# The AV products of two attentions as one group of matmuls, issued where the scores of a later one stand

## The chip, the cores and the metric

The kernel runs on one core of one Trainium2 chip. The metric is the device time of one execution in microseconds, lower is better. Engines are called as in the profile: PE is TensorE (PEld its weight loads), DVE VectorE, ACT ScalarE, POOL GpSimd, SP the queue of SyncE that issues most DMAs. PE multiplies a stationary operand of 128 rows and up to 128 columns, which a weight load puts in place, with a moving operand, and writes to PSUM: eight banks per partition, each of 2 x 256 float32.

## The reference, cut to what matters

A trunk of two layers over 256 positions of width 2048. In each layer one projection feeds a convolution group and an attention group, whose results are gated, concatenated, projected back and added; then an embedding of the layer, gated by the residual, is added. The change lies in the attention group: 16 query heads of width 64 on 4 key/value heads, a window of 128 positions, a bias by relative position, a sink logit per head.

```python
def reference(x, p, norm_g, w_in, ...):
    ...
        u = hn @ w_in[i]
        a_val, a_glu, a_z, q, k, v, b_z = jnp.split(u, offs, axis=-1)
        ...
        yb = _window_attention(q, k, v, bias_band, sink[i]) * jax.nn.silu(b_z)
        h = h + jnp.concatenate([ya, yb], axis=-1) @ w_out[i]
```

Within `_window_attention`:

```python
        s = jnp.einsum('bqkgd,bskd->bkgqs', qb, kb, ...) * scale + bias_band
        m = jnp.maximum(jnp.max(s, axis=-1), sink_f)
        e = jnp.exp(s - m[..., None])
        denom = jnp.sum(e, axis=-1) + jnp.exp(sink_f - m)
        pr = (e / denom[..., None]).astype(vb.dtype)
        return jnp.einsum('bkgqs,bskd->bqkgd', pr, vb)
```

The last line is the AV product, probabilities times values, and the product with `silu(b_z)` follows it.

## The kernel before

Activations lie with channels on the partitions and the 256 positions along the free axis. A projection works through blocks of 128 output columns. Weights come from memory as float32 and are split into two parts, high and low (`split`, L168 on ACT, L171 on DVE); activations are split likewise, and each product of a weight block and an activation block is three matmuls (`mm3`, L401 to L403) of 128x128 by 128x256. The unit of the schedule is a **half**: eight blocks of the contraction, 24 matmuls, one split weight buffer. Two output blocks share one PSUM bank, so a `pair` is four halves.

After each half `pump()` is called. It lets the convolution on DVE go on by some taps, and advances every generator in the list `side` by one `yield`, in the order in which they were put there. The engines PE, DVE and ACT run their instructions in the order in which the program issues them; what a generator issues at a pump therefore stands between two halves of the projection on PE.

Each layer has eight attentions (i = 0 to 7), each for two query heads, hh = 0 and 1. A loop over i in steps of two does a pair of projections for the gate `zb` (its silu is L678), a pair for the queries (`qq`, L685 and L686), and then puts attentions i and i + 1 into `side`, the second to begin four halves after the first. So an attention begins every four halves, and several are under way at a time. After the loop come four pairs of projections `za`, beside which the last attentions run. In halves counted from its beginning, an attention issues:

- 0: the load of its bias (L339, a DMA of POOL)
- 1: scores, eight matmuls into two banks `sc` (L633)
- 2: DVE adds the bias and finds the maxima (L639), ACT follows at 3 with the exponentials (L646), DVE at 4 with the reciprocals (L651), ACT at 5 with the scaling of the probabilities in `s` (L654, four instructions)
- 6: eight transposes of the probabilities into two banks `pt`, one for each hh (L660)
- 7: ACT copies the two banks into two tiles `ptt` (L664)
- 10 (8 for the last one, i = 7): AV, four matmuls in float32 into a bank `av`, of which it uses one half (L670). The values are the stationary operand, 128 rows by 64 columns; the output of hh = 0 goes to partitions 0 to 63 and that of hh = 1 to 64 to 127, so a matmul uses one half of the array's columns. The trace shows each float32 matmul as two instructions: eight per attention
- one half later: DVE multiplies the result into `zb[:, i, :]` (L673)

Step 10 of an attention is step 6 of the next one and step 2 of the one after. On PE the AV of one attention is followed at once by the transposes of the next.

Behind the `za` projections stand `finish` (which pumps until no attention is left), the sums for the normalisation of the convolution (`mean`, L710; `rv0c`, `rv1c`, small matmuls at L354), and the output projections (`o`) and gates (`g`).

Tiles come from pools; a tag with `bufs=n` rotates over n buffers, and a tile waits until the one that had its buffer is read out. The tag `ptt` has two buffers, the tag `u` three: the latter is used at a layer's beginning (`hn`) and in its gates (`hs`). All PSUM banks are one tag of eight buffers.

Of the kernel before, what the change touches and what calls it, by code (L numbers as in the profile page):

```python
# [10 lines left out]
F32 = mybir.dt.float32  # L11
# [6 lines left out]
P = 128  # L18
D = 2048
S = 256  # L20
# [4 lines left out]
HD = 64  # L25
# [44 lines left out]
def backwards(a):  # L70

    (ps, pn), (st, n) = a.ap
    return bass.AP(a.tensor, a.offset + st * (n - 1), [[ps, pn], [-st, n]])
# [56 lines left out]
def trunk_kernel(ctx: ExitStack, tc: tile.TileContext, xT, pT, wst, par, gain, relb, sinkp, onehot, out):  # L130
    nc = tc.nc
# [7 lines left out]
    wk = ctx.enter_context(tc.tile_pool(name="wk", bufs=2))  # L139
# [7 lines left out]
    def halves(t):  # L147
        return [t[:, 0], t[:, 1]]

    def bank(name):  # L150
        return ps.tile([P, 2, S], F32, tag="ps", name=name)
# [85 lines left out]
    def wait(n):  # L237
        for _ in range(n):
            yield
# [94 lines left out]
    def load_bias(i):  # L334

        t = wk.tile([P, 2, 3 * P], F32, name=f"bias{i}", tag="bias", bufs=2)
        base = fscr[2 * i:2 * i + 2, :]
        src = bass.AP(base.tensor, base.offset, [[1, P], [512, 2], [1, 3 * P]])
        nc.gpsimd.dma_start(t, src)  # L339
        return t  # L340
# [98 lines left out]
    for l in range(DEPTH):  # L439
# [32 lines left out]
        for q in range(4):  # L472
# [6 lines left out]
            for jj in range(0, 4, 2):  # L479
                j = 4 * q + jj  # L480
                b = bank("e")
                for x in range(2):
                    for k in range(2):
                        if l:
                            mm3(b[:, x, :], w[:, :, jj + x, k, :], pp[:, :, k, :], x == 0 and k == 0, k == 1)
                        else:
                            nc.tensor.matmul(b[:, x, :], raw[:, jj + x, k, :], pf[:, k, :], start=x == 0 and k == 0,
                                             stop=k == 1, skip_group_check=True)
# [62 lines left out]
        a, zb = halves(az)  # L551
# [62 lines left out]
        v = wk.tile([P, 2, W_KV], F32, name=f"v{l}", tag="v", bufs=1)  # L614
        for b in range(2):
            nc.scalar.copy(v[:, b, :], vb[b][:, 0, :])

        def attention(i, qq, after, l=l, v=v, zb=zb):
            t = i // 4
            yield from wait(after)  # L620
            bias = load_bias(i)
            yield
            nm = wk.tile([P, 2, 2], F32, name="nm", tag="nm")
            den = wk.tile([P, 2, 2], F32, name="den", tag="den")
            es = wk.tile([P, 2, 2], F32, name="es", tag="es")
            sk = sinkt[:, l * NQ + 2 * i:l * NQ + 2 * i + 2].unsqueeze(1).broadcast_to([P, 2, 2])
            each = [(b, hh) for b in range(2) for hh in range(2)]
            o = []
            for b in range(2):
                o.append(bank("sc"))  # L630
                for hh in range(2):
                    for x in range(2):
                        nc.tensor.matmul(o[b][:, hh, :], qq[:, hh, b * P:(b + 1) * P], keys[t][x][:, hh, :],  # L633
                                         start=hh == 0 and x == 0, stop=x == 1, skip_group_check=True)
            yield from wait(1 + AW[0])
            s = [wk.tile([P, 2, S], F32, name="s", tag="s", bufs=4) for b in range(2)]
            for b, hh in each:
                c = l * NQ + 2 * i + hh
                nc.vector.tensor_tensor_reduce(  # L639
                    out=s[b][:, hh, :], in0=o[b][:, hh, :], in1=backwards(bias[:, hh, b * P:b * P + S]),  # L640
                    scale=1.0, scalar=nsink[:, c:c + 1], op0=ALU.add, op1=ALU.min,
                    accum_out=nm[:, b, hh:hh + 1])
            nc.vector.tensor_add(es, nm, sk)
            yield
            for b, hh in each:
                nc.scalar.activation(s[b][:, hh, :], s[b][:, hh, :], AF.Exp, bias=nm[:, b, hh:hh + 1],  # L646
                                     scale=-1.0, accum_out=den[:, b, hh:hh + 1])
            nc.scalar.activation(es, es, AF.Exp)
            yield from wait(1 + AW[1])
            nc.vector.tensor_add(den, den, es)  # L650
            nc.vector.reciprocal(den, den)  # L651
            yield from wait(1 + AW[2])
            for b, hh in each:
                nc.scalar.activation(s[b][:, hh, :], s[b][:, hh, :], AF.Copy, scale=den[:, b, hh:hh + 1])  # L654
            yield from wait(1 + AW[3])
            o = [bank("pt") for hh in range(2)]
            for hh in range(2):
                for b in range(2):
                    for kt in range(2):
                        nc.tensor.transpose(o[hh][:, kt, b * P:(b + 1) * P], s[b][:, hh, kt * P:(kt + 1) * P], ident)  # L660
            yield
            pt = [wk.tile([P, 2, S], F32, name="ptt", tag="ptt") for hh in range(2)]
            for hh in range(2):
                nc.scalar.copy(pt[hh], o[hh])  # L664
            yield from wait(1 if i == 7 else 3)
            o = bank("av")
            for kt in range(2):
                for hh in range(2):
                    g = 2 * t + hh
                    nc.tensor.matmul(o[hh * HD:(hh + 1) * HD, 0, :], v[:, kt, g * HD:(g + 1) * HD], pt[hh][:, kt, :],  # L670
                                     start=(kt == 0), stop=(kt == 1))
            yield
            nc.vector.tensor_mul(zb[:, i, :], o[:, 0, :], zb[:, i, :])  # L673

        for i in range(0, 8, 2):

            b = pair(hg, f"zb{l}_{i}")
            nc.scalar.activation(zb[:, i:i + 2, :], b, AF.Silu)  # L678
            b = pair(hg, f"q{l}_{i}")

            qq = wk.tile([P, 4 * S + 32], F32R, name="qq", tag="qq")
            qq = qq[:, 0:4 * S].rearrange("p (x h s) -> p x h s", x=2, h=2)
            for hh in range(2):
                r, o = rows_of[hh], rows_of[1 - hh]
                nc.scalar.mul(qq[r, :, hh, :], b[r], -(HD ** -0.5))  # L685
                nc.vector.scalar_tensor_tensor(qq[o, :, hh, :], b[r], -(HD ** -0.5), qq[r, :, hh, :].bitcast(F32),  # L686
                                               ALU.mult, ALU.subtract)
            for x in range(2):
                side.append(attention(i + x, qq[:, x], 4 * x))
# [240 lines left out]
```

## Time and profile before

| | us |
|---|---|
| median of 3 runs | 942.69 |
| lowest, highest | 941.69, 943.29 |
| the profiled execution | 943.05 |
| its span, first to last instruction | 941.3 |
| mean granted TensorE clock | 0.996 |

The page of the profile gives busy time by engine, the chain of work that ended last, and groups of instructions by line, with the operand tiles named as out<-in. Other views of the same trace are used below: waits (who waited for whom: total, times, longest), the timeline (start, duration, engine, line, operation, count; neighbours of one group merged), the chain in order of time, and windows (busy time and count of instructions within stretches, with the granted clock, the DMA share and GB/s). Matmuls overlap each other, so their durations add up to more than the time that passes: the spacing of their starts tells what a stream costs.

### The profile page before, as it was taken

To read this page: it belongs to the slowest core of one execution; us is meant where nothing else is said; L and a number is where in the kernel's file an instruction comes from. 1 tells how busy PE (TensorE), PEld (TensorE's weight loads), DVE (VectorE), ACT (ScalarE), POOL (GpSimd) and SP (SyncE) were. 2 spreads that over 40 slices of the span, in tenths; PEclk is the share of its full clock that TensorE was granted. 3 is DMA by queue.
4 is the path that set the end of the run, shared out by engine and by line. 5 is a ranking of instruction groups with operands and counts; after the bars stand their busy time and mean duration, and the time that the engine had idled before them with its cause. 6 is when DMAs were issued, how large, how long until landed. Compare 5 with 4: busy or idle time off the path is not lost.

```text
span 941.3 us, 19132 instructions
## 1 busy us (share of the span) xinstructions
PE 928.9 (99%) x7968; PEld 912.3 (97%) x7968; DVE 767.9 (82%) x1290; ACT 550.3 (58%) x830; POOL 83.0 (9%) x79
## 2 busy tenths in 40 slices
PE   8999999999999999999999999999999999999995
PEld 7999999999999999999999999999999999999995
DVE  3999999998787786786679999999887877777663
ACT  4655455787874555554467445568778546445551
POOL 0023001010000000011102100000100000000111
PEclk9999999999999999999999999999999999999999
DMA  8674556555546456556545556566455554655532
GB/s 296 230 253 162 197 180 237 191 202 186 171 158 249 156 213 211 189 180 232 212 183 205 183 198 222 179 213 201 170 169 180 176 206 146 257 179 180 198 117 90
DMA packets 29011, 182.55 MB, mean 194 GB/s; under 512 B 3595, under 2 KB 4156, under 8 KB 9084
## 3 DMA queue, kind: packets, MB, share of 16 engines
q1 hardware_dynamic: 24284, 165.70, 49.7%
q0 software_dynamic: 3344, 12.88, 4.2%
q10 hardware_dynamic: 1296, 2.75, 0.8%
q8 instruction: 62, 1.02, 0.4%
q14 instruction: 25, 0.20, 0.1%
HBM read 177.09 MB, written 4.23 MB: 193 GB/s over the span
## 4 chain that ended last, share of the span: by engine, by line
PE 95%; DVE 2%; DMA 1%; ACT 1%; issue 0%; ACTq 0%; DVEq 0%
PE o L401 6%; PE o L402 6%; PE o L403 6%; PE ag L401 6%; PE g L403 6%; PE ag L403 6%; PE ag L402 6%; PE g L402 6%; PE g L401 6%; PE za L401 3%; PE za L403 3%; PE za L402 3%; PE zb L401 3%; PE zb L403 3%; PE zb L402 3%; PE q L401 3%
## 5 line engine op out<-in xcount | busy, mean ns | idle before, releaser
L171 DVE TENSOR_TENSOR w<-raw,w 128x1024 fp32r<-128x1024 f32 x306 | 374.4, 1232 | 101.4 <-ACT w L168 100.4
L168 ACT CAST w<-raw 128x1024 fp32r<-128x1024 f32 x308 | 316.2, 1046 | 156.6 <-PE ag L403 44.0
L565 DVE SCALAR_TENSOR_TENSOR cz<-az,pars,cz 128x241 f32<-128x241 f32 (+11 forms) x480 | 216.2, 500 | 1.0
L401 PE MATMUL ag<-hg,w 128*128 128x256 f32 x512 | 141.9, 277 | 0.0
L403 PE MATMUL g<-h,w 128*128 128x256 f32 x512 | 141.5, 276 | 0.0
L402 PE MATMUL ag<-hg,w 128*128 128x256 f32 x512 | 141.5, 276 | 0.0
L403 PE MATMUL ag<-hg,w 128*128 128x256 f32 x512 | 141.5, 276 | 0.0
L401 PE MATMUL g<-h,w 128*128 128x256 f32 x512 | 141.4, 276 | 0.0
L402 PE MATMUL g<-h,w 128*128 128x256 f32 x512 | 141.4, 276 | 0.0
L401 PEld LDWEIGHTS ag<-hg,w 128*128 128x128 f32 x512 | 96.1, 188 | 0.9 <-ACT w L168 0.8
L402 PEld LDWEIGHTS ag<-hg,w 128*128 128x128 f32 x512 | 96.2, 188 | 0.0
L402 PEld LDWEIGHTS g<-h,w 128*128 128x128 f32 x512 | 96.1, 188 | 0.0
L403 PEld LDWEIGHTS ag<-hg,w 128*128 128x128 f32 x512 | 96.1, 188 | 0.0
L401 PEld LDWEIGHTS g<-h,w 128*128 128x128 f32 x512 | 96.1, 188 | 0.0
L403 PEld LDWEIGHTS g<-h,w 128*128 128x128 f32 x512 | 96.1, 188 | 0.0
L401 PE MATMUL za<-hg,w 128*128 128x256 f32 x256 | 71.9, 281 | 0.0
L401 PE MATMUL q<-hg,w 128*128 128x256 f32 x256 | 71.9, 281 | 0.0
L401 PE MATMUL o<-yb,w 128*128 128x256 f32 x256 | 71.9, 281 | 0.0
L401 PE MATMUL zb<-hg,w 128*128 128x256 f32 x256 | 71.5, 279 | 0.0
L402 PE MATMUL q<-hg,w 128*128 128x256 f32 x256 | 71.4, 279 | 0.0
L403 PE MATMUL q<-hg,w 128*128 128x256 f32 x256 | 71.4, 279 | 0.0
L402 PE MATMUL o<-yb,w 128*128 128x256 f32 x256 | 71.3, 278 | 0.0
(227 smaller groups left out, 2273.0 us busy)
## 6 DMA issues: line engine op xcount, KB each, us to landing
raw<-in_wst SPq DMA_DIRECT2D x153, 1024.0 KB, 4.9
bias<-fscr POOLq DMA_DIRECT2D x16, 384.0 KB, 3.9
raw<-in_wst SPq DMA_DIRECT2D x4, 512.0 KB, 7.9
az<-in_xT POOLq DMA_DIRECT2D x4, 512.0 KB, 5.6
hscr<-e POOLq DMA_DIRECT2D x2, 1024.0 KB, 5.6
az<-hscr POOLq DMA_DIRECT2D x4, 512.0 KB, 5.4
x<-in_xT SPq DMA_DIRECT2D x3, 512.0 KB, 8.2
out_t<-og ACTq DMA_DIRECT2D x4, 256.0 KB, 3.0
```

Source lines behind the costliest of these rows:

```text
L168: nc.scalar.copy(hi, raw)
L171: nc.vector.tensor_sub(lo, raw, hi.bitcast(F32))
L401: nc.tensor.matmul(o, w[:, 0], x[:, 0], start=start, stop=False, skip_group_check=True)
L402: nc.tensor.matmul(o, w[:, 0], x[:, 1], start=False, stop=False, skip_group_check=True)
L403: nc.tensor.matmul(o, w[:, 1], x[:, 0], start=False, stop=stop, skip_group_check=True)
L565: nc.vector.scalar_tensor_tensor(acc[:, t, lo_:hi_], a[:, t, lo_ + s:hi_ + s], w(k), acc[:, t, lo_:hi_], ALU.mult, ALU.add)
```

## The change

AV is done for two attentions at a time. The transposed probabilities are handed over in a list, `probs`, one list per layer. An attention with even i ends after the copies. One with odd i takes both pairs of tiles from the list and issues eight AV matmuls (sixteen instructions) into one bank, the even attention into its first half and the odd one into its second; one DVE product of 128x512 replaces two of 128x256. The matmul that starts accumulation is flagged so only for the first attention, since the flag acts on the whole bank. The odd attention does this at its half 9 (8 for i = 7, as before), which is half 1, the scores, of the attention two later. The tiles `ptt` of odd attentions take the tag `u`.

```diff
+        probs = []
+
-        def attention(i, qq, after, l=l, v=v, zb=zb):
+        def attention(i, qq, after, l=l, v=v, zb=zb, probs=probs):
...
-            pt = [wk.tile([P, 2, S], F32, name="ptt", tag="ptt") for hh in range(2)]
+            pt = [wk.tile([P, 2, S], F32, name="ptt", tag="u" if i % 2 else "ptt", bufs=3 if i % 2 else 2)
+                  for hh in range(2)]
             for hh in range(2):
                 nc.scalar.copy(pt[hh], o[hh])
-            yield from wait(1 if i == 7 else 3)
+            probs.append(pt)
+            if i % 2 == 0:
+                return
+            yield from wait(1 if i == 7 else 2)
             o = bank("av")
-            for kt in range(2):
-                for hh in range(2):
-                    g = 2 * t + hh
-                    nc.tensor.matmul(o[hh * HD:(hh + 1) * HD, 0, :], v[:, kt, g * HD:(g + 1) * HD], pt[hh][:, kt, :],
-                                     start=(kt == 0), stop=(kt == 1))
+            for x in range(2):
+                pt = probs.pop(0)
+                for kt in range(2):
+                    for hh in range(2):
+                        g = 2 * t + hh
+                        nc.tensor.matmul(o[hh * HD:(hh + 1) * HD, x, :], v[:, kt, g * HD:(g + 1) * HD],
+                                         pt[hh][:, kt, :], start=x == 0 and kt == 0, stop=kt == 1,
+                                         skip_group_check=True)
             yield
-            nc.vector.tensor_mul(zb[:, i, :], o[:, 0, :], zb[:, i, :])
+            nc.vector.tensor_mul(zb[:, i - 1:i + 1, :], o, zb[:, i - 1:i + 1, :])
```

## The prediction

> **What bounds the kernel now.** I read the page first: busy time, then the chain that ended last.
>
> ```profile
> span 941.3 us, 19132 instructions
> PE 928.9 (99%) x7968; PEld 912.3 (97%) x7968; DVE 767.9 (82%) x1290; ACT 550.3 (58%) x830; POOL 83.0 (9%) x79
> PE 95%; DVE 2%; DMA 1%; ACT 1%; issue 0%; ACTq 0%; DVEq 0%
> ```
>
> TensorE (PE) is the bound: 99% busy, 95% of the chain. The waits of PE, all of them in the span, come next; the second row is the only one in the attention stage.
>
> ```profile
> PE warm L261 <- DVE zeros L258: 1.2, 1, 1.2
> PE sc L633 <- DVE qq L686: 0.3, 1, 0.3
> ```
>
> So no engine is to be relieved here. What counts is how PE's stream is spaced, and a busy share can't show that, since matmuls overlap. I therefore read start times in the timeline of PE. This is the second attention's AV with the third's transposes; columns are start, duration, what.
>
> ```profile
> 206.61 0.28 PE L402 MATMUL q<-hg,w 128*128 128x256 f32 x1
> 206.73 0.28 PE L403 MATMUL q<-hg,w 128*128 128x256 f32 x1
> 206.94 1.08 PE L670 MATMUL av<-ptt,v 128*64 128x256 f32 x8
> 207.95 1.09 PE L660 MATMUL pt<-ident,s 128*128 128x128 f32 x8
> 209.00 0.28 PE L402 MATMUL q<-hg,w 128*128 128x256 f32 x1
> ```
>
> Projection matmuls start 0.12 apart. The first AV one starts 0.21 behind its predecessor, not 0.12: a price for entering 64-column tiles ("128*64"). From 206.73 to the second projection matmul behind the group (209.00) are 2.27 us; two steps (0.23) would have passed anyway, so AV with transposes costs **2.04**. The same stage has transposes alone (first attention) and AV alone (last one):
>
> ```profile
> 179.10 0.28 PE L403 MATMUL q<-hg,w 128*128 128x256 f32 x1
> 179.22 1.04 PE L660 MATMUL pt<-ident,s 128*128 128x128 f32 x8
> 180.22 0.28 PE L402 MATMUL q<-hg,w 128*128 128x256 f32 x1
> ...
> 283.80 0.28 PE L403 MATMUL za<-hg,w 128*128 128x256 f32 x1
> 284.01 1.08 PE L670 MATMUL av<-ptt,v 128*64 128x256 f32 x8
> 285.25 0.28 PE L402 MATMUL za<-hg,w 128*128 128x256 f32 x1
> ```
>
> Transposes alone: 1.12 - 0.23 = **0.89**. AV alone: 1.45 - 0.23 = **1.22**.
>
> One more thing must be seen: **the step of PE's stream has two lengths**. The windows view, PE alone, over stretches that hold projections only; the x is the count of matmuls.
>
> ```profile
> 593.00:621.00 28.00, 28.00 (x240) 1.00 0.69 240
> 843.00:871.00 28.00, 28.00 (x249) 1.00 0.51 180
> ```
>
> The granted clock is 1.00 in both. About two counted matmuls only reach into a window, so a step lasts 28.00/247 = 0.1134 in one and 28.00/238 = 0.1176 us in the other. I call them short and long step. A half (24 matmuls, the unit of the schedule) takes 24 x 0.0042 = 0.10 us more at long step. Equal windows of 5.2 us through the attention stage:
>
> ```profile
> 183.00:188.20 5.20, 5.20 (x48) 1.00 0.63 195
> 197.60:202.80 5.20, 5.20 (x46) 1.00 0.71 244
> 211.70:216.90 5.20, 5.20 (x48) 1.00 0.51 191
> 225.70:230.90 5.20, 5.20 (x46) 1.00 0.90 280
> ...
> 278.60:283.80 5.20, 5.20 (x46) 1.00 0.59 208
> 287.00:292.20 5.20, 5.20 (x49) 1.00 0.66 255
> 297.60:302.80 5.20, 5.20 (x47) 1.00 0.61 237
> 319.00:324.20 5.20, 5.20 (x48) 1.00 0.60 205
> ```
>
> 46 or 47 is the long step, 48 or 49 the short one. The length changes at small groups of matmuls, which the chain of waits places:
>
> ```profile
> 192.71 1.01 PE av L670 x8
> 203.24 0.95 PE sc L633 x8
> 207.01 1.01 PE av L670 x8
> 220.91 1.01 PE av L670 x8
> 293.47 1.29 PE mean L710 x6
> 308.96 0.79 PE rv0c L354 x8
> ```
>
> Each AV group turns it over: short to long at 192.71, long to short at 207.01, and so on; AV alone at 284.01 too. Transposes alone at 179.22 leave it short. The scores at 203.24 leave it long (206.61 to 206.73 is still 0.12). The mean at 293.47 turns it long, rv0c at 308.96 ends that. Long halves of a layer: four behind each of three AV groups, two before 284.01, five between mean and rv0c: 19. I have no mechanism for it, only this pattern.
>
> **The change part by part.** An attention issues scores, transposes and AV at its steps 1, 6 and 10; a new one starts every 4 steps. Today AV of one falls into the step of the next one's transposes. After: an even attention stops at its copies; an odd one issues both AVs at step 9, where the attention two later issues its scores, behind them in the list. The last pair's stands alone at step 8.
>
> *Groups on PE.* The matmuls are the same ones; only borders go. Per layer before: 0.89 + 7 x 2.04 + 1.22 = 16.39 us. After: eight times transposes alone, 8 x 0.89 = 7.12, and four AV groups of double length. How long is a doubled one? The trace has none. Within a group of eight, starts come in pairs:
>
> ```profile
> 207.20 0.82 PE L670 MATMUL av<-ptt,v 128*64 128x256 f32 x6
> ...
> 207.42 0.60 PE L670 MATMUL av<-ptt,v 128*64 128x256 f32 x4
> ```
>
> Two matmuls less take 0.22 less: the two column halves run side by side, one slot per pair. (The mean, 1.29/6 = 0.215 per matmul, gives the slot more finely.) Four more slots are 4 x 0.215 = 0.86; ends: 0.86 if they run in pairs, 1.72 if one by one. I take 0.86, since the order of the halves within an attention is unchanged. A group costs 1.22 + 0.86 = 2.08, four 8.32, the layer 15.44. **Gain 0.95 per layer, 1.9 in all.** The border from AV to scores is not in the trace: it lies between that to projections (nothing off) and that to transposes, where the pair costs 2.04 against 0.89 + 1.22 = 2.11, 0.07 less. Three per layer: 0 to 0.4 us more gain in all. I take nothing, because scores have the shape of projections (128*128, 256 columns; the row at 203.24 gives 0.95/8 = 0.119 each, no border at all). So standing next to the scores is worth nothing in itself.
>
> By the Trainium skill, "TensorEngine Tiling (Array Packing)", section Key Properties, changing the tiling mode drains TensorE, so 16 of 32 changes would go. "TensorE: Matmul & The Clock Gate", section Single matmul latency, gives 166 ns warm as the constant that an isolated matmul cannot hide; as an estimate 16 x 0.166 = 2.7 us, where the rows above give 1.9, and the rows decide.
>
> *Step length.* Here the size of the result is settled, and the trace bounds it only from both sides. At best the doubled group leaves the step short: 14 long halves fewer per layer (the five behind the mean stay), 2.8 us in all. At worst the step is long from the first doubled group (now three halves later) up to rv0c: 31 halves instead of 19, 2.4 us more. I take: a doubled group makes the step long, as AV does, and the transposes one half later end it, as every group other than scores that met a long step did. Long halves: 1 behind each of three groups, 3 behind the last, 5 behind the mean: 11 instead of 19, 8 x 0.10 x 2 = **1.6 us gain**.
>
> *VectorE.* Sixteen products become eight of double width; the second row is another PSUM addition of that width.
>
> ```profile
> L673 DVE TENSOR_TENSOR az<-av,az 128x256 f32<-128x256 f32 x16 | 6.7, 418 | 0.0
> L758 DVE TENSOR_TENSOR az<-o,az 128x512 f32<-128x512 f32 x16 | 11.0, 685 | 0.9 <-PE o L403 0.9
> ```
>
> 6.7 - 8 x 0.685 = 1.2 us less on an engine that PE does not wait for: nothing. If that cover were gone, this would be the gain.
>
> *Waits.* Odd transposes come earlier, since no AV stands before them, and they need ScalarE's scaling. The tightest places, ScalarE first:
>
> ```profile
> 190.91 1.71 ACT L654 ACTIVATE s<-s,den 128x256 f32<-128x256 f32 x4 [0.69 <-DVE den L651]
> 192.64 1.08 PE L670 MATMUL av<-ptt,v 128*64 128x256 f32 x8
> ...
> 274.13 1.71 ACT L654 ACTIVATE s<-s,den 128x256 f32<-128x256 f32 x4 [0.69 <-DVE den L651]
> 276.31 1.08 PE L670 MATMUL av<-ptt,v 128*64 128x256 f32 x8
> ```
>
> The transposes move to where AV starts today. Scaling ends at 192.62, they start at 192.64; at the last attention 275.84 against 276.31, less what PE is ahead by then. That just holds: the last of the four scalings is needed by the seventh transpose only. Behind a waiting transpose the whole projection stream would stand. AV has two steps behind its copies instead of three, the scores come 2.08 later behind AV but VectorE reads them a step later: nothing. The longer-held transposed tiles of odd attentions go to a three-deep tag idle in this stage; PSUM turns over 11 banks per pair instead of 12. No DMA moves on SP; POOL's load of the next p waits for the last AV at an unchanged step.
>
> Sum: 1.9 + 1.6 = 3.5 us. The profiled execution took 943.05 (span 941.3 and 1.75 around it): 939.5. It lies 0.36 above the median of the runs, so I say **939.2** against 942.69.
>
> **The rivals.**
>
> *The doubled group leaves the step short.* For it: doubling something that turns the step over may turn it twice. Against: the mean too, with slots of the same length, makes it long. 1.9 + 2.8 = 4.7: 938.0.
>
> *Step length as often long as now.* Each doubled group turns it over once, and transposes leave it: 7 to 8 halves between groups, 15 long ones where there were 14. 1.9 - 0.2 = 1.7: 941.0. The skill's rule of the drain, which knows no length of step behind a group, would leave 1.9: 940.8.
>
> *The step stays long up to rv0c.* 2.4 - 1.9 = 0.5 worse: 943.2. For it: only the groups named above were seen to end a long step, and transposes alone never met one.
>
> *Odd transposes wait.* If each of the eight stands for the quarter of a microsecond that its pair gains at the borders (1.9/8), that gain is gone, and with the step length as now: about 942.8.
>
> *Slower: nothing ends the long step.* If rv0c, met in another phase, doesn't end it either, the output and gate projections run long as well, 59 halves (the 64 of both stages without the five that are long now): with the 12 above 71 more per layer, 142 x 0.10 = 14.2 - 1.9 = 12.3 worse, 955.0. It decides from 19 extra long halves (1.9 us). Against it: rv0c ended a long step in this layer (297.60 against 319.00).
>
> **How the numbers follow.** About 0.2% (1.9 us, so 940.8 and 944.6) is what a measurement of this kernel can tell from no change. Chances: forecast 0.34, short step throughout 0.28, as often long as now 0.20 (0.06 of it beyond the bound), long up to rv0c 0.09, waiting transposes 0.05, slower 0.04. Faster 0.34 + 0.28 + 0.06 = 0.68, same 0.14 + 0.09 + 0.05 = 0.28, slower 0.04. The range takes the first three cases with half a microsecond for the border to the scores and the scatter of the runs: 937.4 to 941.6; 0.18 is left out.
>
> **What would show it.** Right: eight groups of transposes alone at 0.89, four AV groups of sixteen matmuls lasting 1.08 + 0.86 = 1.94, seven fewer borders between AV and transposes per layer, eight products of about 0.69, and projection windows of 48 to 49 nearly everywhere up to the mean. Wrong: AV groups of 2.8 us (halves one by one), PE rows that wait for L654, or windows of 46 through whole pairs; the last would make the gain 1.7 or nothing, while the borders still go.

## The result, and the profile after

| | before | after |
|---|---|---|
| median, us | 942.99 | **938.42** |
| lowest to highest (4 runs each) | 941.69 to 943.39 | 937.63 to 939.89 |
| ratio to before, 95% interval | | 0.9957 [0.9945, 0.9969] |
| the profiled execution, us | 943.05 | 937.63 |
| its span, us | 941.3 | 935.9 |

The medians in this document leave out three executions that took far longer than the rest: two of e1's five (1331 and 5341 us) and one of the kernel before beside it (2414 us). The kernel is faster by 4.57 us by the medians; the interval of the ratio is 2.9 to 5.2 us of 942.99. The profiled execution of after is the lowest of its four, so the traces differ by a little more than the medians: 5.4.

First the page of after, the same rows as of before: busy time and instructions by engine, then the shares of the chain that ended last.

```profile
span 935.9 us, 19124 instructions
PE 923.6 (99%) x7968; PEld 910.3 (97%) x7968; DVE 767.6 (82%) x1282; ACT 548.9 (59%) x830; POOL 82.4 (9%) x79
PE 95%; DVE 2%; DMA 1%; ACT 1%; issue 0%; POOL 0%; ACTq 0%; DVEq 0%
```

PE issues the same 7968 matmuls, is just as busy and still has 95% of the chain. Only eight DVE instructions are gone. The waits view of PE has the same one row in the attention stage as before, and the groups view has the eight products of double width at the duration that was forecast (about 0.69 each):

```profile
PE sc L635 <- DVE qq L695: 0.3, 1, 0.3
...
L682 DVE TENSOR_TENSOR az<-av,az 128x512 f32<-128x512 f32 x8 | 5.5, 682 | 0.0
```

So nothing waits that did not wait before. The same work fits into less time because it is spaced more closely. Where that happens is read from the chain in order of time: the first scores of a layer and the first small matmuls behind its attention stage (rv0c, rv1c) bracket the stage. Before (layer 1 ends with the row at 308.96, shown in the prediction):

```profile
163.85 0.95 PE sc L633 x8
...
621.30 0.95 PE sc L633 x8
...
765.88 0.79 PE rv1c L354 x8
```

After, with the first doubled AV group and the two scores next to it:

```profile
163.61 0.96 PE sc L635 x8
...
201.60 1.88 PE av L678 x16
203.47 1.14 PE sc L635 x8
...
216.43 0.95 PE sc L635 x8
...
306.19 0.79 PE rv0c L354 x8
...
618.53 0.95 PE sc L635 x8
...
760.46 0.79 PE rv1c L354 x8
```

| stretch | before | after | gained |
|---|---|---|---|
| up to the first scores of layer 1 | 163.85 | 163.61 | 0.24 |
| attention stage of layer 1 | 145.11 | 142.58 | 2.53 |
| between the stages | 312.34 | 312.34 | 0.00 |
| attention stage of layer 2 | 144.58 | 141.93 | 2.65 |

The two stages give 5.18 us. The 0.24 ahead of the first attention isn't the change's doing; it is scatter, which e5 comes back to.

**Borders.** The timeline of PE in after: start, duration, engine and line, what. The first rows are a doubled AV group with scores behind it, then transposes alone, then the last AV group, alone.

```profile
201.32 0.28 PE L403 MATMUL q<-hg,w 128*128 128x256 f32 x1
201.53 1.95 PE L678 MATMUL av<-ptt,v 128*64 128x256 f32 x16
...
204.58 0.28 PE L402 MATMUL q<-hg,w 128*128 128x256 f32 x1
...
207.09 0.28 PE L403 MATMUL q<-hg,w 128*128 128x256 f32 x1
207.21 1.03 PE L662 MATMUL pt<-ident,s 128*128 128x128 f32 x8
...
208.20 0.28 PE L402 MATMUL q<-hg,w 128*128 128x256 f32 x1
...
280.34 0.28 PE L403 MATMUL za<-hg,w 128*128 128x256 f32 x1
280.55 1.95 PE L678 MATMUL av<-ptt,v 128*64 128x256 f32 x16
...
282.65 0.28 PE L402 MATMUL za<-hg,w 128*128 128x256 f32 x1
```

The length of a group is worked out as in the prediction: last projection matmul ahead of the group to the second one behind it, less two steps (0.23). AV alone: 2.31 - 0.23 = 2.08. Transposes alone: 1.11 - 0.23 = 0.88. AV with scores: 3.26 - 0.23 = 3.03, and scores alone take 0.95 (the row at 216.43), so AV costs 2.08 here too: the price of leaving the 64-column tiles shows up in the scores (1.14 behind AV against 0.95).

**Step length.** Windows of PE alone, 5.2 us each, projections only; as in the prediction, 46 or 47 matmuls are the long step, 48 or 49 the short one.

```profile
195.60:200.80 5.20, 5.20 (x48) 1.00 0.60 192
210.60:215.80 5.20, 5.20 (x48) 1.00 0.75 245
223.50:228.70 5.20, 5.20 (x48) 1.00 0.65 199
...
285.40:290.60 5.20, 5.20 (x47) 1.00 0.70 219
295.20:300.40 5.20, 5.20 (x48) 1.00 0.73 246
```

The stage is short nearly throughout. Behind the doubled group with scores (201.53) the starts are 0.12 and then 0.11 apart again, and the window that follows is short. Only the last AV group, which stands alone, makes the step long (285.40), for three halves up to the mean. Behind the mean the starts are still 0.12 apart; then comes one spacing of 0.18, a few matmuls into the output projection, and only behind that is the step short (295.20):

```profile
293.13 0.34 PE L402 MATMUL o<-yb,w 128*128 128x256 f32 x1
293.31 0.28 PE L403 MATMUL o<-yb,w 128*128 128x256 f32 x1
```

The kernel before has the same spacing of 0.18 at that place (295.43 to 295.61), and its step stays long behind it. With one half behind the scores at 188.75, which had waited for their queries, layer 1 has 4 long halves; layer 2 has 3. There were 19 in each.

The account closes: 0.95 for borders and 15 x 0.10 = 1.5 for the step make 2.45 in layer 1 (2.53 measured), 0.95 and 16 x 0.10 = 1.6 make 2.55 in layer 2 (2.65). But the five halves behind the mean in each layer, 1.0 us in all, can't be put down to the change. In the twelve profiles of this document, before, after and e1 to e10, that spacing stands behind every mean, 24 times; the step behind it is short 14 times and long ten times. Four of the profiles (e1, e3, e4, e7) have one outcome in one layer and the other in the other layer.

### The profile page after: what moved, and what is told of

Read it like the earlier page. It is cut to its first block, busy times and chain, and to the rows that moved or that the text cites. A ratio compares the mean times of both kernels' runs of the same rounds, so it can differ in the third digit from the quotient of the medians.

```text
span 935.9 us, 19124 instructions
## 1 busy us (share of the span) xinstructions
PE 923.6 (99%) x7968; PEld 910.3 (97%) x7968; DVE 767.6 (82%) x1282; ACT 548.9 (59%) x830; POOL 82.4 (9%) x79
## 4 chain that ended last, share of the span: by engine, by line
PE 95%; DVE 2%; DMA 1%; ACT 1%; issue 0%; POOL 0%; ACTq 0%; DVEq 0%
PE ag L401 6%; PE ag L402 6%; PE ag L403 6%; PE o L401 6%; PE o L402 6%; PE o L403 6%; PE g L403 6%; PE g L402 6%; PE g L401 6%; PE za L401 3%; PE za L403 3%; PE za L402 3%; PE zb L403 3%; PE zb L401 3%; PE zb L402 3%; PE q L401 3%
## 5 line engine op out<-in xcount | busy, mean ns | idle before, releaser
L401 PE MATMUL za<-hg,w 128*128 128x256 f32 x256 | 71.7, 280 | 0.0
L401 PE MATMUL o<-yb,w 128*128 128x256 f32 x256 | 71.4, 279 | 0.0
L401 PE MATMUL q<-hg,w 128*128 128x256 f32 x256 | 71.4, 279 | 0.0
L401 PE MATMUL zb<-hg,w 128*128 128x256 f32 x256 | 71.3, 279 | 0.0
L403 PE MATMUL zb<-hg,w 128*128 128x256 f32 x256 | 71.0, 277 | 0.0
L402 PE MATMUL zb<-hg,w 128*128 128x256 f32 x256 | 71.0, 277 | 0.0
L403 PE MATMUL za<-hg,w 128*128 128x256 f32 x256 | 71.0, 277 | 0.0
```

What stands on the lines that cost most here:

```text
L401: nc.tensor.matmul(o, w[:, 0], x[:, 0], start=start, stop=False, skip_group_check=True)
L402: nc.tensor.matmul(o, w[:, 0], x[:, 1], start=False, stop=False, skip_group_check=True)
L403: nc.tensor.matmul(o, w[:, 1], x[:, 0], start=False, stop=stop, skip_group_check=True)
```

## The experiments

What was open: why the doubled group leaves the step short. Is it the doubling, or that scores stand behind AV where transposes stood? The expectations number the theories for e1 to e4. Theory 1: only the borders count. Theory 2: a group of double length leaves the step short, whatever stands behind it. Theory 3: what stands behind AV decides; scores leave the step short, transposes or projections don't. In e6 to e9, A and B name two theories that each expectation states for itself. Three sets of runs were made, each beside runs of the kernel before:

| run | median, us | before | ratio, 95% |
|---|---|---|---|
| e1: doubled AV beside transposes | 938.58 | 942.85 | 0.9959 [0.9942, 0.9976] |
| e2: doubled AV alone | 939.62 | 942.85 | 0.9965 [0.9952, 0.9978] |
| e3: single AV beside scores | 941.29 | 942.85 | 0.9981 [0.9972, 0.9991] |
| e4: changed kernel, two products | 938.63 | 942.85 | 0.9956 [0.9940, 0.9972] |
| e5: changed kernel again | 939.15 | 942.47 | 0.9961 [0.9947, 0.9975] |
| e6: two transposes more, five places | 938.96 | 942.47 | 0.9961 [0.9948, 0.9973] |
| e7: one narrow matmul more, same places | 938.61 | 942.47 | 0.9961 [0.9949, 0.9974] |
| e8: AV alone, 1 to 4 transposes behind | 941.06 (one run) | 942.47 | |
| e9: kernel before, with work added | 942.35 | 942.16 | 1.0003 [0.9994, 1.0012] |
| e10: two transposes more, three places | 937.44 | 942.16 | 0.9956 [0.9943, 0.9968] |

The totals of most differ by less than their scatter. The trace of each is what tells the theories apart.

### Where the doubled AV stands: e1, e2, e3

e1 and e2 are the changed kernel with the doubled AV a half later (in front of transposes) or a half earlier (between projections). e3 is the kernel before with its single AV a half earlier, in front of scores.

```diff
# e1
-            yield from wait(1 if i == 7 else 2)
+            yield from wait(1 if i == 7 else 3)
# e2
-            yield from wait(1 if i == 7 else 2)
+            yield from wait(1)
# e3
-            yield from wait(1 if i == 7 else 3)
+            yield from wait(1 if i == 7 else 2)
```

> The doubled AV group one half later, directly ahead of the transposes of the next attention instead of ahead of the scores. Theory 1 (the borders are all that changed): one border per group becomes cheaper by 0.07, six of them, so 0.4 us below the changed kernel, about 938.0. Theory 2 (a group of double length leaves the step of PE's stream short, whatever follows it): no long step behind the first three groups of a layer, the same 938.0. Theory 3 (what follows AV decides: transposes make the step long, scores don't): windows of 46 behind each group, four halves until the next transposes, 24 halves x 0.10 = 2.4 slower, 940.4, or eight halves until the next AV, 4.8 slower, 942.8.

> The doubled AV group one half earlier, alone between two halves of a projection. Theory 1 (borders only): the scores had no border of their own, so nothing changes, 938.4. Theory 2 (a double group leaves the step short): 938.4, although the last group of each layer, which stands alone, was followed by windows of 46. Theory 3 (the neighbour decides): long step as behind that last group, two halves until the next transposes, 12 x 0.10 = 1.2 slower, 939.6; if transposes don't end it, eight halves, 938.4 + 4.8 = 943.2.

> The kernel before, AV of one attention at a time as there, but one half earlier, so that it stands ahead of the scores of the attention two later and no longer ahead of transposes. Theory 1 (borders only): 14 borders lose the 0.07 that AV and transposes saved together, 1.0 slower than before, about 944.0. Theory 2 (the double length is what keeps the step short): single groups go on turning the step over, 14 long halves per layer as before, 944.0. Theory 3 (scores behind AV keep the step short): the long halves of the attention stage go, 28 x 0.10 = 2.8 faster than that, about 941.2.

e1, window of PE behind the first doubled group of layer 1 with transposes:

```profile
211.00:216.20 5.20, 5.20 (x49) 1.00 0.79 265
```

Short, and so it is behind the other five such groups of the two layers. A doubled AV with transposes behind it leaves a short step short, where a single one with transposes made it long. So **theory 3 falls** here: behind a doubled AV, transposes don't make the step long.

e2, windows of 2.6 us (23 or 24 is long, 25 or 26 short) at the first group, behind the doubled AV alone and behind the transposes two halves later:

```profile
201.30:203.90 2.60, 2.60 (x23) 1.00 0.79 325
208.80:211.40 2.60, 2.60 (x25) 1.00 0.34 110
```

Alone, the same sixteen matmuls make the step long, in all six such groups of e2. So **theory 2 falls** as well: double length by itself does not settle it. Theory 3 is right for this run, in the windows and in the time (939.62 measured, 939.6 expected). Theory 1 has no room for any of this: e2 has the borders of the changed kernel, yet its attention stages take 143.6 and 143.0 us against 142.6 and 141.9 (half of this difference lies behind the mean). So neither AV nor its neighbour decides alone; the two together do.

The transposes two halves later end the long step, six times of six here, as the prediction had assumed. In the twelve profiles they ended 21 of the 24 long steps that they met. The three that they left long (in e1, e4 and e7) are all at the second transposes of layer 1, behind the scores that had waited for their queries.

e3, windows behind single AV groups with scores (190.50, 204.40, 218.40), and behind the transposes that follow the third one (221.90):

```profile
190.50:193.10 2.60, 2.60 (x25) 1.00 0.01 3
204.40:207.00 2.60, 2.60 (x26) 1.00 0.46 101
218.40:221.00 2.60, 2.60 (x24) 1.00 0.19 28
221.90:224.50 2.60, 2.60 (x25) 1.00 0.80 337
```

Of its twelve such groups six left the step short and six made it long, each time for one half only, up to the next transposes. The kernel gets to the 941.2 that theory 3 gave, but by another way: not because scores always keep the step short, but because the transposes that end a long step come sooner. In each layer the kernel before has four long halves behind three of its AV groups and two behind a fourth. Altogether e3 has 6 and 13 long halves in its two layers, against 19 and 19. This is worth having by itself: one number changed in a wait gives 1.6 us (942.85 - 941.29), with no border removed.

### VectorE, and the scatter: e4, e5

e4 is the changed kernel with its product in two instructions again; e5 is the changed kernel unedited.

```diff
-            nc.vector.tensor_mul(zb[:, i - 1:i + 1, :], o, zb[:, i - 1:i + 1, :])
+            for x in range(2):
+                nc.vector.tensor_mul(zb[:, i - 1 + x, :], o[:, x, :], zb[:, i - 1 + x, :])
```

> The changed kernel with VectorE's product split again into one of 128x256 per attention, 1.2 us more of VectorE in all. All theories: nothing, 938.4, since PE waits for no product. If the shorter VectorE time was part of the gain: up to 1.2 slower, 939.6.

> The changed kernel once more, on the chip of the next three, as their measure and to see which long steps come back from one execution to the next. If the step is set by the program alone: the same windows as in its first profile, short behind the three double groups ahead of scores, long behind the last one, short behind the mean. If it also hangs on when PE had to wait before: stretches behind a wait (the first projections, those behind the scores at 189 us that wait for the queries) come out otherwise. Time 938.4 in both cases.

938.63 against 938.42 for the changed kernel: the merged product is worth nothing that can be seen. e4's trace shows the price of the step once more. In layer 1 the transposes at 192.43 left the step long, and so did the doubled group with scores that met it there; in layer 2 the step stayed long behind the mean. It has 8 and 8 long halves where after has 4 and 3, and its stages are 0.4 and 0.5 us longer.

e5 repeats the pattern of the first profile: short behind every doubled group with scores, the last group long, short behind the mean in both layers. Only the half behind the scores that wait for their queries, long in after, is short in e5. The ratio, 0.9961, lies within the first one's interval; by its medians the gain is 3.3 us (942.47 - 939.15), against 4.57 the first time. The two profiled executions of this one kernel differ by 1.5 us, and all of that lies ahead of the first scores, which start at 163.61 in after and at 165.19 in e5. The windows of 20 to 28 us, first after, then e5:

```profile
20.00:28.00 8.00, 8.00 (x55) 1.00 0.62 213
```
```profile
20.00:28.00 8.00, 8.00 (x44) 0.84 0.52 187
```

The granted clock is 1.00 in one and 0.84 in the other, with 11 matmuls fewer, 11 x 0.1176 = 1.3 us. The step adds to the scatter: from 28 to 48 us, far ahead of the change, the kernel before has 179 matmuls and after and e5 have 172, 7 x 0.1176 = 0.8 us, half of the forecast's whole step term. e2, the changed kernel with one wait altered, has 179 there too.

### Can the long halves that are left be ended? e6, e7, e10

Layer 2's gate and query projections ahead of its first scores still run long for ten halves in before and after alike. In e6 two transposes of the identity, whose results nobody reads, are added at five places of the changed kernel: in the first gate projection of layer 2, behind the last AV of both layers, and behind the first output projection half, after the mean, of both layers. e7 puts a matmul of one column there instead, e10 leaves out the two places after the mean.

```diff
+    def nudge(n=2):
+        nb = bank("nudge")
+        for _ in range(n):
+            nc.tensor.transpose(nb[:, 0, 0:P], ident, ident)
...
+            if nudged and x == 0:
+                nudge()
...
+            if i == 7:
+                nudge()
...
+                if j == 0 and x == 0:
+                    nudge()
```

> The changed kernel with two transposes of the identity added, whose result nobody reads, at five places where the step was long or may become so: behind the first half of the second layer's gate projection (long for ten halves in all profiles so far), directly behind the last AV group of each layer (long for three halves), and behind the first half after the mean. Cost 5 x 0.22 = 1.1 us. Theory A (transposes end or prevent a long step): nine halves there, three twice, up to four twice: at best 23 x 0.107 = 2.5 gained, 1.4 below the changed kernel, about 937.0, without the mean about 937.9. Theory B (the length of the whole group matters, not that there are transposes; the eight transposes ended it by chance): windows of 46 stay, 1.1 above, 939.5.

> The same five places with a single matmul of one column (two instructions, some 0.22 us) instead of two transposes; rv0c and rv1c, eight such instructions, ended long steps in all profiles. Theory A (any disturbance of other shape ends a long step): as with two transposes, 937.0 to 937.9. Theory B (the length of the group matters): some end it and some don't, 938 to 939.5, and the windows tell which.

> The changed kernel with the two added transposes kept only where they ended or prevented a long step: in the second layer's gate projection and behind the last AV group of each layer, not behind the mean. Cost 3 x 0.22 = 0.7 us; nine halves and twice three become short, 15 x 0.107 = 1.6. If nothing else comes late: 0.9 below the changed kernel, about 938.0. If PE, earlier by a microsecond, now waits for the queries ahead of the second layer's third scores, as it did with the five places: 0.2 to 0.5 of that is given back, 938.3 to 938.5.

e10, windows over layer 2's gate and query projections, and behind the last AV of layer 1:

```profile
592.80:617.80 25.00, 25.00 (x222) 1.00 0.67 240
282.80:285.40 2.60, 2.60 (x26) 1.00 0.95 258
```

The changed kernel's profile has 215 in the first of these stretches:

```profile
593.20:618.20 25.00, 25.00 (x215) 1.00 0.69 240
```

So two transposes end the long step there, and they keep the step short behind the last AV of both layers. It is hardly worth anything: in layer 2, PE now comes about 1 us sooner to the third scores, and finds their queries not ready. The timeline of e10 (in square brackets the wait, and on what):

```profile
641.99 0.28 PE L643 MATMUL sc<-keys0l,qq 128*128 128x256 f32 x1
642.49 0.39 PE L643 MATMUL sc<-keys0h,qq 128*128 128x256 f32 x1 [0.22 <-DVE qq L705]
```

These eight scores, 0.95 without a wait, take 1.46 here: half of the gain goes into a new wait. After the mean, where the step was short already, e6's two transposes turned it long for four halves in each layer; this is the reason for e10. Neither theory's time for e6 (937.0 to 937.9, or 939.5) was met: 938.96.

```profile
295.30:300.50 5.20, 5.20 (x46) 1.00 0.58 219
```

e7 came out as its theory B says, in the time (938.61) and in the windows. Its narrow matmul ended the long step in the gate projection of layer 2 and behind the mean of layer 1, but behind the last AV the step was long in both layers (24 and 24 matmuls in 2.6 us). e10 has the lowest median of all, 937.44, but its interval, 0.9943 to 0.9968, holds the 0.9961 of the changed kernel's repeat: the two are not told apart.

### How long must a group be? e8, e9

e8 takes e2, whose doubled AV alone made the step long, and adds one, two, three and four transposes of the identity behind the four groups of a layer, results unread. e9 adds one such transpose in layer 1 and two in layer 2 to the kernel *before*, behind its transposes beside AV: 7 x 1 + 7 x 2 = 21 matmuls of pure waste.

```diff
# e8
+            nudge((i + 1) // 2)
# e9, behind the transposes
+            if i:
+                nudge(1 + l)
```

> The doubled AV group alone between projections, as in the experiment with the pair alone, where each was followed by the long step until the next transposes; behind the four groups of a layer stand 1, 2, 3 and 4 transposes of the identity that nobody reads (0.11 each, 2.2 us in all). Theory A (transposes behind AV, however few, leave the step short): windows of 48 behind all four. Theory B (the length of the whole group matters): short behind some numbers and long behind others, the same in both layers. Time about 939.6 + 2.2 less 0.2 to 0.4 per group kept short: 939.5 to 941.8.

> The kernel before (AV of one attention at a time, ahead of the next one's transposes) with useless transposes of the identity behind those transposes, wherever AV stands before them: one in each of seven groups of the first layer (7 x 0.11 = 0.8 us), two in the second (7 x 0.22 = 1.5). Nothing is taken away and no border goes. Theory 1 (borders and matmuls are all that PE's stream costs): 2.3 us slower than before, 945.3. Theory B (the length of a group decides how long the step is behind it): a layer in which the new length leaves the step short loses its 14 long halves, 1.5 us: first layer 0.7 faster in spite of the added work, second layer even; 942.2 if both do, 943.7 or so if one does. The windows of each layer tell.

e8, windows behind the four groups of layer 1, then of layer 2:

```profile
201.30:203.90 2.60, 2.60 (x25) 1.00 0.66 271
228.90:231.50 2.60, 2.60 (x25) 1.00 0.69 290
256.70:259.30 2.60, 2.60 (x25) 1.00 0.52 202
283.80:286.40 2.60, 2.60 (x24) 1.00 0.85 255
657.40:660.00 2.60, 2.60 (x25) 1.00 0.43 183
685.20:687.80 2.60, 2.60 (x25) 1.00 0.64 268
713.10:715.70 2.60, 2.60 (x25) 1.00 0.38 158
740.00:742.60 2.60, 2.60 (x24) 1.00 0.46 164
```

None (e2): long. One, two, three: short. Four: long again, in both layers. It isn't the place: behind the last group of a layer, where the four stand, two (e6, e10) leave the step short. So it is not that there are transposes, but how many, as theory B has it, and the step turns more than once as the group grows. Whether length alone decides is not shown, and e7 speaks against it: its group behind the last AV, 2.30 us, left the step long, though it lies between 2.26 (two transposes, short) and 2.36 (three, short). The total, 941.06 in one run, tells little by itself: the added transposes are paid for in it, and four of them end nothing.

e9, the added group on PE, and windows behind two of its groups:

```profile
L430 PE MATMUL nudge<-ident 128*128 128x128 f32 x21 | 4.6, 273 | 0.0
...
197.20:202.40 5.20, 5.20 (x48) 1.00 0.75 244
225.10:230.30 5.20, 5.20 (x48) 1.00 0.83 277
```

21 matmuls more, which at 0.11 each (0.88/8) are 2.3 us of PE, the bound, and the time stays the same: 942.35 against 942.16, 1.0003 [0.9994, 1.0012]. Theory B gave 942.2, theory 1 945.3. The windows at 197.20 and 225.10, behind AV with eight transposes and one more, have 48 where the kernel before has 46; all 14 groups left the step short. What the added matmuls cost, the shorter step pays back: there are 4 and 3 long halves instead of 19 and 19, 31 x 0.10 = 3.1 us, of which ten halves (1.0) are those behind the mean. This is the clearest proof that the step length is a term of its own: it moved by more than 2 us in the kernel *before*, with its borders, its order and its sixteen products all kept.

## Why the prediction was right, point by point

- **PE is the bound and nothing else is relieved:** as forecast. PE has 95% of the chain in both, and e4 shows that the merged product is worth nothing.
- **Borders, 0.95 a layer, 1.9 in all:** as forecast, term by term: AV group 2.08 (2.08 forecast), transposes alone 0.88 (0.89). The doubled group runs its column halves side by side (1.95 for sixteen against 1.08 for eight; 1.94 forecast). The border from AV to the scores, bounded by 0 and 0.4 and taken as nothing, is nothing: AV with scores costs 2.08 + 0.95. The prediction's estimate by the Trainium skill, 2.7 ("TensorE: Matmul & The Clock Gate", section Single matmul latency), was above what the rows gave, and the rows held. What the rows give can be taken apart: a group between projections takes 0.36 more than its slots (1.22 - 4 x 0.215, and 2.08 - 8 x 0.215), and eight such groups fewer would be 2.9; but 14 of the groups before stood beside transposes, where the pair cost 0.07 less, so 1.0 of that had been saved already.
- **Waits:** none came, as forecast. No row of the waits of PE names the scaling that the odd transposes need.
- **Step length:** right in kind, wrong in size; this is the term that was mis-sized. The prediction took it that "a doubled group makes the step long, as AV does, and the transposes one half later end it", 11 long halves a layer, 1.6 us gained. The second part is right, with few exceptions (e2, and 21 of 24 in all profiles). The first is right only for a doubled group that stands alone (e2, and the last group in both profiles of the changed kernel). Beside scores it leaves a short step short, so 3 of the 11 halves never came, and the 5 behind the mean were short too. 4 and 3 long halves were measured, worth 15 x 0.10 + 16 x 0.10 = 3.1 us instead of 1.6.
- **What of this was luck:** the ten halves behind the mean, 1.0 of the 3.1 us. Behind the 0.18 us spacing there, the step is short in some profiles and long in others, with the change and without it.
- **The sum:** 1.9 + 3.1 = 5.0 from the terms as measured, 5.18 between the brackets of the two traces, 4.57 between the medians (3.3 in e5), 3.5 forecast. The rival "the doubled group leaves the step short", 4.7 us and 938.0, describes the chain of events better than the forecast does. It took the group itself for the reason, though, where e2 shows that the group and what stands behind it decide together. The stated range covered the forecast and this rival both, so that the time fell into it does not tell them apart; the windows do.
- **The mistake behind it:** the prediction read "Each AV group turns it over" from a trace in which every AV group but the last of a layer stood in front of eight transposes. AV and what stands behind it could not be told apart there, and "standing next to the scores is worth nothing in itself" is true of the border alone: in e2, without the scores, each of the six groups is followed by two long halves, 12 x 0.10 = 1.2 us. The text also excepts scores from the groups that end a long step, but in the same trace the first scores of layer 2 (621.30) met a long step and left a short one, as they did in all nine profiles where they met one.
- **The slower rival** (nothing ends the long step) had no chance to show: the step was short at nearly every point where it would have begun.

## What to carry to other kernels

Where the engine that is the bound is 99% busy in both kernels, read the spacing of its starts: count matmuls in equal windows that hold one kind of work. Small groups put between a dense stream can cost more, or less, than their own duration, because the stream behind them may run at another pace; try the group one slot earlier or later and count again before you make its work smaller. Profile one kernel twice before you credit a change with a stretch that runs faster. And when PE gets ahead by a microsecond, look for the next operand that is now late: in e10 half of the gain went into a wait for queries that had just been in time.

## What the runs showed of the hardware

- At a granted clock of 1.00, the same stream of matmuls runs at 0.1134 or 0.1176 us a step. The difference, 0.10 us per 24 matmuls, made 3.1 of the 5.0 us of this change.
- The step mostly turns at a small group of other matmuls, but not only there: in after it turns from short to long between two projections of layer 2 (at 590.1), and from long to short at the single spacing of 0.18 us behind the mean.
- Which step follows goes with what the group consists of. Lengths below are worked out from the timelines as in the paragraph on borders, for groups that met a short step, in all twelve profiles:

| group | length, us | step behind it |
|---|---|---|
| eight transposes | 0.89 | short 130 times, long 4 |
| AV of one | 1.22 | long (6) |
| AV of one, eight transposes | 2.04 | long (8) |
| AV of two | 2.08 | long (16) |
| AV of one, nine or ten transposes | 2.15, 2.27 | short (13) |
| AV of two, one to three transposes | 2.15, 2.26, 2.36 | short (10) |
| AV of one, scores | 2.17 | six short, six long |
| AV of two, one narrow matmul (e7) | 2.30 | long (2) |
| AV of two, four transposes | 2.47 | long (2) |
| AV of two, eight transposes | 2.91 | short (6) |
| AV of two, scores | 3.03 | short (34) |

- Groups of nearly equal length agree in most rows, but the rows at 2.17 and 2.30 lie among short ones, so length alone is not the rule. Nor does it explain the scores: 0.95 us each, they left a long step long between the AV groups of the kernel before and short at the beginning of layer 2. Why the step turns stays open.
- A group that met a long step often left a short one: AV of one with eight transposes six times of six, the small matmuls rv0c and rv1c 11 of 11. AV of two with scores left it long, twice of two (e4, e7).
- Part of the scatter between executions lies far ahead of the change: a granted clock of 0.84 instead of 1.00 from 20 to 28 us (1.3 us), and one step or the other in the first projections (0.8 us).
